# Three one-row reads on the store ring, and one table copy moved from POOL to ScalarE, in a rotary-embedding kernel

**Chip and metric.** One core of one Trainium2 chip. The metric is the device time of one execution in microseconds (us), lower is better; all runs quoted are of state fast unless it is said otherwise. The profile's span is 1.76 to 1.83 us shorter than this time for the kernel before. In the profiles SP is the engine SyncE, ACT ScalarE, DVE VectorE, PE TensorE and POOL GpSimd; the ring is the queue of transfers that SP has issued and the DMA engines have not yet done.

## The reference

```python
half = x.shape[-1] // 2                      # x: (8, 8, 1024, 64) float32, 16.8 MB
x_first, x_second = x[..., :half], x[..., half:]
out_first  = x_first * cos_cached - x_second * sin_cached      # tables: (1024, 32)
out_second = x_first * sin_cached + x_second * cos_cached
return np.concatenate([out_first, out_second], axis=-1)
```

Every element is read once and written once, so 16.8 MB come in and 16.8 MB go out, beside two tables of 128 KB.

## The kernel before

x is cut into eight units of 128 partitions x 4096 elements (2 MB). All loads and all stores are issued by SP, the loads at the very start. The tables come in as 32 partitions; their even rows are spread to 128 partitions by TensorE, their odd rows by a shuffle on VectorE and three copies of 32-partition quadrants. VectorE then does most of the multiplying, and POOL and TensorE most of the adding and subtracting.

```python
nc.sync.dma_start(out=rs, in_=sin_cached...)          # sine table, SP
nc.scalar.dma_start(out=rc, in_=cos_cached...)        # cosine table, ACT's queue
for m0, m1 in ((0, F // 2), (F // 2, F)):             # unit 0 in two halves
    nc.sync.dma_start(out=xt[0][:, m0:m1], in_=xf[0][:, m0:m1])
for u in range(1, n_u):                               # units 1 to 7
    nc.sync.dma_start(out=xt[u], in_=xf[u])
# ... cut: helpers
for t, r in ((sn, rs), (cs, rc)):
    nc.vector.stream_shuffle(t[0:Q, H:], flat(r), odd)          # odd table blocks, quadrant 0
nc.scalar.copy(out=tb4[Q:2 * Q, H:], in_=tb4[0:Q, H:])          # quadrant 1: ScalarE
for k in range(2, P // Q):
    nc.gpsimd.tensor_copy(out=tb4[k*Q:(k+1)*Q, H:], in_=tb4[0:Q, H:])   # 2 and 3: POOL
mul(nc.vector, rows(sv[0], 0, H), ..., tab(flat(en), 0, H))     # unit 0, even half
# ... cut: two more products from PSUM
pool_sums(0, 0, H, sv[7])
stage(pre, 0, H, R)                                   # ScalarE: unit 0, odd half, into PSUM `pre`
nc.scalar.copy(out=sn[:, :H], in_=flat(en))           # even table blocks
# ... cut
products(pre, 0, H, R)                                # VectorE: needs `pre` and the odd blocks
# ... cut: the other units, and behind them
store(0); store(1); ...; store(6)                     # SP, 2 MB each
store(7, 0, 24); store(7, 24, 48); store(7, 48, 64)
```

## Time and profile before

| what | before | from |
|---|---|---|
| time, median of 6 runs | 85.28 us (85.18 to 85.71) | runs |
| queue 1 (SP's) on its 16 DMA engines | 95.5% of 83.6 us | DMA queues |
| VectorE, POOL busy | 82%, 80% | busy times |
| first store issued, landed | 21.76, 48.2 us | timeline, DMA issues |
| last store issued | 75.96 us; the span ends at 83.6 | timeline |

How to read it: a transfer has two times, the issue on SP's timeline and the landing, and between them it may stand in the ring behind others. The lines are in the prediction below.

### The profile page before, as it was taken

How to read it: one execution, taken by the hardware profiler on the slowest of the kernel's cores; microseconds unless marked ns; L12 is line 12 of the kernel's file. 1: busy time of each engine (PE TensorE's matmuls, PEld its weight loads, DVE VectorE, ACT ScalarE, POOL GpSimd, SP SyncE). 2: the span in 40 equal slices, each digit the busy share in tenths (PEclk: the TensorE clock that was granted, in tenths of full speed). 3: DMA queues.
4: the chain of work that ended last, by engine and by line, in shares of the span. 5: the costliest groups of instructions: out<-in, count | busy, mean ns of one | idle time of the engine just before them, and what ended most of it. 6: DMA issues, size and time to landing. Idle time of an engine off the chain costs nothing.

```text
span 83.6 us, 386 instructions
## 1 busy us (share of the span) xinstructions
PE 44.1 (53%) x80; PEld 16.9 (20%) x80; DVE 68.5 (82%) x30; ACT 40.7 (49%) x36; POOL 67.2 (80%) x36
## 2 busy tenths in 40 slices
PE   0199930004993694949769494961994970000000
PEld 0143300002430332405133240411340410000000
DVE  0193999999999999999999999999999998940000
ACT  4409694464068548196176856675266526000000
POOL 3009909999999999999999999999999999991000
PEclk9999999999999999999999999999579999655555
DMA  1999999999999999999999898999999999999990
GB/s 18 308 415 447 435 431 447 392 470 407 423 447 407 454 400 439 439 415 447 384 423 454 384 486 384 478 400 454 423 400 470 392 478 392 470 400 394 423 425 20
DMA packets 2833, 33.82 MB, mean 404 GB/s; under 512 B 337, under 2 KB 337, under 8 KB 785
## 3 DMA queue, kind: packets, MB, share of 16 engines
q1 hardware_dynamic: 2784, 33.69, 95.5%
q10 hardware_dynamic: 48, 0.13, 0.4%
q14 instruction: 1, 0.00, 0.0%
HBM read 17.04 MB, written 16.78 MB: 404 GB/s over the span
## 4 chain that ended last, share of the span: by engine, by line
POOL 63%; issue 13%; PE 4%; DMA 4%; DVE 3%; POOLq 2%
POOL w L109 26%; POOL w L110 24%; POOL w L106 14%; PE en L156 4%; DMA w<-in_sin_cached_dram 4%; DVE w L106 3%; POOLq L258 2%; POOLq L109 0%; POOLq L106 0%
## 5 line engine op out<-in xcount | busy, mean ns | idle before, releaser
L106 DVE TENSOR_TENSOR w<-st,tb 128x3072 f32<-128x3072 f32 (+2 forms) x19 | 54.7, 2956 | 0.3 <-ACT st L113 0.3
L113 ACT COPY st<-w 128x1536 f32<-128x1536 f32 (+1 forms) x19 | 24.9, 1310 | 15.7 <-DVE w L106 14.6
L184 PE MATMUL acc<-w,plus 128*128 128x512 f32 x36 | 21.4, 679 | 20.4 <-ACT w L190 11.4
L109 POOL TENSOR_TENSOR w<-w 128x1024 f32<-128x1024 f32 (+3 forms) x11 | 23.9, 2169 | 0.2
L110 POOL TENSOR_TENSOR w<-w 128x1024 f32<-128x1024 f32 (+3 forms) x11 | 23.8, 2166 | 0.0
L184 PEld LDWEIGHTS acc<-w,plus 128*128 128x128 f32 x36 | 6.9, 215 | 33.9 <-ACT w L190 18.0
L190 ACT COPY w<-acc 128x1024 f32<-128x1024 f32 x9 | 9.1, 1010 | 8.5 <-PE acc L185 8.5
L106 POOL TENSOR_TENSOR w<-w,tb 128x1280 f32<-128x1280 f32 x4 | 11.7, 2921 | 0.2
L185 PE MATMUL acc<-w,minus 128*128 128x512 f32 x18 | 10.9, 690 | 0.0
L185 PE MATMUL acc<-w,plus 128*128 128x512 f32 x18 | 9.2, 592 | 0.0
L162 POOL COPY tb<-tb 32x2048 f32<-32x2048 f32 x2 | 3.8, 1888 | 5.2 <-DVE tb L159 5.2
L156 PE MATMUL en<-w,sel 32*128 32x512 f32 x4 | 3.7, 1089 | 3.9 <-DMA w<-in_sin_cached_dram 3.9
L185 PEld LDWEIGHTS acc<-w,minus 128*128 128x128 f32 x18 | 4.0, 223 | 5.4 <-issue 5.4
L106 DVE TENSOR_TENSOR w<-pre,tb 128x4096 f32<-128x4096 f32 x1 | 4.4, 4418 | 0.0
L185 PEld LDWEIGHTS acc<-w,plus 128*128 128x128 f32 x18 | 3.4, 190 | 4.4 <-issue 4.4
L109 POOL TENSOR_TENSOR w<-w,w 128x1024 f32<-128x1024 f32 x1 | 2.4, 2361 | 2.2 <-issue 2.2
L156 PE MATMUL ec<-w,sel 32*128 32x512 f32 x4 | 3.6, 1056 | 0.0
L160 ACT COPY tb<-tb 32x2048 f32<-32x2048 f32 x1 | 1.9, 1897 | 3.4 <-DVE tb L159 3.4
L106 DVE TENSOR_TENSOR w<-w,en 128x2048 f32<-128x2048 f32 x1 | 2.3, 2289 | 1.4 <-PE en L156 1.4
L159 DVE LOAD_MASK_SELECT tb<-w x2 | 0.0, 8 | 3.8 <-DMA w<-in_sin_cached_dram 3.8
L159 DVE STREAM_SHUFFLE tb<-w 32x1024 f32<-32x1024 f32 x2 | 2.5, 1282 | 0.0
L106 DVE TENSOR_TENSOR w<-w,ec 128x1024 f32<-128x1024 f32 x2 | 2.4, 1218 | 0.0
(18 smaller groups left out, 14.2 us busy)
## 6 DMA issues: line engine op xcount, KB each, us to landing
w<-in_x_dram SPq DMA_DIRECT2D x7, 2048.0 KB, 24.9
out_dram<-w SPq DMA_DIRECT2D x7, 2048.0 KB, 10.5
w<-in_x_dram SPq DMA_DIRECT2D x2, 1024.0 KB, 6.4
out_dram<-w SPq DMA_DIRECT2D x2, 768.0 KB, 6.7
out_dram<-w SPq DMA_DIRECT2D x1, 512.0 KB, 6.7
w<-in_cos_cached_dram ACTq DMA_DIRECT2D x1, 128.0 KB, 3.3
w<-in_sin_cached_dram SPq DMA_DIRECT2D x1, 128.0 KB, 3.1
```

The source lines that it names most:

```text
L106: eng.tensor_tensor(out=o, in0=a, in1=t, op=TT.mult)
L109: eng.tensor_tensor(out=o[:, :, 0], in0=c[:, :, 0], in1=s[:, :, 1], op=TT.subtract)
L110: eng.tensor_tensor(out=o[:, :, 1], in0=c[:, :, 1], in1=s[:, :, 0], op=TT.add)
L113: nc.scalar.copy(out=pt[:, :(n1 - n0) * hd], in_=xt[u][:, n0 * hd:n1 * hd])
L156: nc.tensor.matmul(part, sel, r, start=True, stop=True)
L159: nc.vector.stream_shuffle(t[0:Q, H:], flat(r), odd)
L160: nc.scalar.copy(out=tb4[Q:2 * Q, H:], in_=tb4[0:Q, H:])
L162: nc.gpsimd.tensor_copy(out=tb4[k * Q:(k + 1) * Q, H:], in_=tb4[0:Q, H:])
L184: nc.tensor.matmul(a[:, k], plus, xr[:, :, k], start=True, stop=False)
L185: nc.tensor.matmul(a[:, k], plus if k else minus, sr[:, :, 1 - k], start=False, stop=True)
L190: nc.scalar.copy(out=rows(xt[u], n0, n0 + G), in_=a)
L258: with _tile.TileContext(nc) as tc:
```

## The change

The three row reads fill a tile that nothing uses. The intent, as far as the diff shows it, is to put something between loads and stores on SP's ring, and to balance the copies between POOL and ScalarE.

```diff
     for u in range(1, n_u):
         nc.sync.dma_start(out=xt[u], in_=xf[u])
+    row = const.tile([1, 3 * hd], fp32, name="row")
+    for i in range(3):
+        nc.sync.dma_start(out=row[:, i * hd:(i + 1) * hd], in_=xf[i][0:1, 0:hd])
@@
-        nc.scalar.copy(out=tb4[Q:2 * Q, H:], in_=tb4[0:Q, H:])
-        for k in range(2, P // Q):
-            nc.gpsimd.tensor_copy(out=tb4[k * Q:(k + 1) * Q, H:], in_=tb4[0:Q, H:])
+        for k in range(1, P // Q):
+            copy = nc.gpsimd.tensor_copy if k == 1 else nc.scalar.copy
+            copy(out=tb4[k * Q:(k + 1) * Q, H:], in_=tb4[0:Q, H:])
```

## The prediction

> **What bounds the kernel now.** I read the page's slices first. Of the engines and the DMA, the row that is never under eight tenths from the second slice to the last but one is the one to suspect.
>
> ```profile
> DVE  0193999999999999999999999999999998940000
> POOL 3009909999999999999999999999999999991000
> DMA  1999999999999999999999898999999999999990
> GB/s 18 308 415 447 435 431 447 392 470 407 423 447 407 454 400 439 439 415 447 384 423 454 384 486 384 478 400 454 423 400 470 392 478 392 470 400 394 423 425 20
> ```
>
> VectorE (DVE) and POOL both look full, but both stop some 8 us before the span ends (a slice is 83.6/40 = 2.09 us). DMA goes on to the last slice but one, and its GB/s swings about one level from slice 3 to the end. So I take the DMA queues next, and in them the share of sixteen engines' span.
>
> ```profile
> q1 hardware_dynamic: 2784, 33.69, 95.5%
> HBM read 17.04 MB, written 16.78 MB: 404 GB/s over the span
> ```
>
> Queue 1 (SP's) keeps all sixteen DMA engines busy for 95.5% of 83.6 us, 79.8 us. What is left, 3.8 us, is the start before the first bytes move, the landing of the last ones, and under half a microsecond of gaps. No engine's order of work can shorten the 79.8 us, since neither its bytes nor its rate depend on it. The chain of the page names another culprit:
>
> ```profile
> POOL 63%; issue 13%; PE 4%; DMA 4%; DVE 3%; POOLq 2%
> ```
>
> It follows semaphores from the last instruction back and ends at about 75.5 us; the 8 us after that are transfers already in the ring, so its 63% is not a bound. Whether POOL matters is asked of the stores: is each one in the ring before the engines get to it? The DMA issues give the median landing, and single stretches of the same view give single ones.
>
> ```profile
> w<-in_x_dram SPq DMA_DIRECT2D x7, 2048.0 KB, 24.9
> out_dram<-w SPq DMA_DIRECT2D x7, 2048.0 KB, 10.5
> ```
>
> A 2 MB transfer takes 2.097 MB / 429 GB/s = 4.9 us by itself (a 16 KB packet takes 611 ns on one of sixteen engines, which is that rate). That stores take 10.5 us from issue to landing means that they stand behind others for the rest. The first store, and the one with the least room:
>
> ```profile
> 21.76 0.35 SPq L142 DMA_DIRECT2D out_dram<-w  x1
> ...
> out_dram<-w SPq DMA_DIRECT2D x1, 2048.0 KB, 26.4
> ...
> 69.51 0.33 SPq L142 DMA_DIRECT2D out_dram<-w  x1
> ```
>
> The first was issued at 21.76 and landed at 48.2, 4.9 us after the last load (issued at 6.6, 36.7 to landing: 43.3). So stores do not overtake loads. The store of unit 6 was issued at 69.51; the packets place its first byte at about 71.8. An issue needs 1.1 us to its first packet (sine table: issued at 0.74, first packet at about 1.8), so it could come some 1.2 us later before the DMA ran dry. For the other stores the same subtraction gives 2 us or more.
>
> **What the Trainium skill says.** (1) "DMA: Bandwidth & Descriptors", Specifications, gives 16 engines and a fabric ceiling of 435 GB/s. The trace agrees: 424 to 433 GB/s in stretches from 9 to 76 us, at a full DMA share. (2) The same page, Queues, rings and completion order: on each DMA engine descriptors are consumed in ring order. The first store's 26.4 us agrees. (3) The same page, Why a DMA increments its semaphore by 16: the number of DMA engines used follows the slowest dimension that is not 1. For a row of 64 elements that could be 16 pieces of 16 B, or one of 256 B if the row is carried whole; no transfer in this trace has one partition, so the trace does not tell. (4) Specifications also says that below 512 B a transfer becomes a read-modify-write. The trace has only the 4 B semaphore writes as transfers below 512 B (9 ns each), so a penalty on data is not shown; it is my main doubt.
>
> **The change, part by part.**
>
> *Row reads on the ring.* They carry 3 x 256 B. Queue 1 spends 79.8 us x 16 = 1277 us of engine time on 33.69 MB, 38 ns per KB, so 256 B should take about 10 ns, and with a small packet's fixed cost some 20 ns. The semaphore write adds 9 ns. If one engine carries a row, three cost it 3 x 29 = 87 ns; if sixteen do, each pays perhaps 3 x 18 = 54 ns. I put +0.05 us on the end.
>
> *Semaphores.* The built order shows what the diff does not: SP's transfers share eight completion semaphores in rotation, and a transfer that takes a semaphore again first waits for its last user. Before, the first store took over from the second half of unit 0; now the three rows take over from that half and from units 1 and 2, and every store moves on by three. The first store waits for unit 3's load, the second for unit 4's, the third to fifth for those of units 5, 6 and 7, the later ones for the rows and for the first two stores. Loads land 4.9 us apart: unit 1 at 14.0, unit 3 at 23.8, unit 4 at 28.7, unit 7 at 43.3. The first store therefore goes out at about 23.9 instead of 21.76. The second was issued at 35.39 against a landing at 28.7, the third at 47.90 against 33.6, the fifth at 57.12 against 43.3: no wait. The first store's 2.1 us cost nothing, since the ring has loads until 43.3. The rows stand behind all the loads and land at about 43.5 to 44.
>
> *Quadrant copies.* Timeline of the start, one engine after the other:
>
> ```profile
> 6.34 1.90 ACT L160 COPY tb<-tb 32x2048 f32<-32x2048 f32 x1 [3.36 <-DVE tb L159]
> 9.12 1.87 ACT L113 COPY pre<-w 128x2048 f32<-128x2048 f32 x1 [0.88 <-DMA w<-in_x_dram]
> 11.02 1.01 ACT L169 COPY tb<-en 128x1024 f32<-128x1024 f32 x1
> 11.93 1.08 ACT L171 COPY tb<-ec 128x512 f32<-128x512 f32 x2
> ...
> 9.92 2.43 DVE L106 TENSOR_TENSOR w<-w,ec 128x1024 f32<-128x1024 f32 x2
> 12.27 4.42 DVE L106 TENSOR_TENSOR w<-pre,tb 128x4096 f32<-128x4096 f32 x1
> ...
> 6.46 3.82 POOL L162 COPY tb<-tb 32x2048 f32<-32x2048 f32 x2 [5.15 <-DVE tb L159]
> 12.49 2.36 POOL L109 TENSOR_TENSOR w<-w,w 128x1024 f32<-128x1024 f32 x1 [2.22 <-issue]
> ```
>
> POOL loses one copy of 1.89 us and is done at 8.35 instead of 10.28. It gains nothing: its first sum needs VectorE's products, which end at 9.92 + 2.43 = 12.35, so its idle time grows from 2.2 to 4.1 us. ScalarE (ACT) gets a second copy of 1.9 us. Of that, 0.88 us falls into its wait for the second half of unit 0. Its copies end at 6.34 + 3.8 = 10.1, the stage into `pre` ends at 12.0 instead of 10.99, and VectorE's products from `pre` may start after that. VectorE was not free before 12.27, so the delay is 0 to 0.1 us. The table copies from PSUM then end at 14.0 to 14.1, and the next stage, which waited for unit 1 until 14.07, starts at most 0.1 us later; VectorE wants it only at 16.6. So the path sees 0 to 0.1 us, and the tightest store's 1.2 us swallow it.
>
> Sum: 85.28 + 0.05 + 0 = 85.33 us.
>
> **The rivals.**
> (a) *The rotated waits hold stores back.* For it: two or three semaphores guard a store, and an early store does wait 2.1 us longer. Against it: each new predecessor lands many microseconds before its store is ready, except for the first store, which stands behind loads anyway. If the ring were not in order and the early store had filled holes, a gap of 2 us would come up: 87.4.
> (b) *Short reads stall a DMA engine.* For it: the read-modify-write of the skill, and the rows adjoin. If each of three rows holds the lowest engine for a round trip (the smallest transfers of the trace need 3.1 us to landing, of which some 2 us are no data), every later store waits for that engine: up to 6 us, 87 to 91. Against it: packets on one engine follow each other without a pause in the trace, latency included.
> (c) *VectorE starts later.* It runs without a break from 7.7 to 70, so a delay in `pre` travels to the last store. If ScalarE's copies became slower beside POOL's, by 0.5 us each, it would start 1 us late and still lie inside the 1.2 us: 85.3 to 85.6.
> (d) *Faster.* An earlier POOL could bring stores forward, but the DMA has them waiting already; only fewer bytes or a higher rate would help. 85.2 at best.
>
> **Range and chances.** The runs before lie within 85.21 to 85.71, and another chip or moment moves by as much. I take 85.0 to 85.8 around 85.33. Slower by over 2% means a DMA gap of 1.7 us, which only (a) or (b) makes: 0.025. Faster by over 2% needs 1.7 us out of 3.8 us of start, gaps and landing that the change does not touch: 0.01. The rest, 0.965, is the same.
>
> **What would show it.** Right: queue 1 still at 95% or so and no empty slice; the first store issued near 23.9 and landing near 48.3; the others issued within 0.2 us of before; the rows landing at 43 to 44, after the last load; POOL's idle before its first sum near 4 us; the products from `pre` starting at 12.2 to 12.4. Wrong: a slice under eight tenths of DMA near 43 us (rival b) or between two stores (a); a store whose issue is released by a transfer; products from `pre` after 13 us.

## The result

85.38 us median (85.23 to 85.53, 6 runs) against 85.28. The ratio is 1.0007, 95% interval 0.9986 to 1.0029: the same time. A ratio here is the mean time of one kernel's runs over the mean of the other's of the same rounds, so it is not quite the ratio of the medians.

The page of the changed kernel, its DMA slices and its queue 1 (packets, MB, share of sixteen engines), and the chain it names:

```profile
DMA  2999989999999999999999999999999999998991
GB/s 47 260 409 440 480 378 440 440 417 464 385 456 417 433 448 393 472 393 440 440 394 480 385 440 440 417 464 393 472 393 440 440 417 456 393 480 368 425 407 75
q1 hardware_dynamic: 2790, 33.69, 96.0%
POOL 64%; issue 10%; DVE 6%; PE 5%; DMA 4%; POOLq 2%
```

The DMA is full from end to end as before. Queue 1 has six packets more, three rows and three semaphore writes. The DMA issues (size, median us to landing), then the timeline of SP's issues in three stretches (start, us taken), then one landing:

```profile
w<-in_x_dram SPq DMA_DIRECT2D x7, 2048.0 KB, 29.2
out_dram<-w SPq DMA_DIRECT2D x7, 2048.0 KB, 10.5
row<-in_x_dram SPq DMA_DIRECT2D x3, 0.2 KB
...
9.03 10.02 SPq L88 DMA_DIRECT2D row<-in_x_dram  x3
23.79 0.38 SPq L147 DMA_DIRECT2D out_dram<-w  x1
69.53 0.33 SPq L147 DMA_DIRECT2D out_dram<-w  x1
...
out_dram<-w SPq DMA_DIRECT2D x1, 2048.0 KB, 24.4
```

The first store was issued at 23.79, two microseconds later than before, and landed at 48.2, when it had landed before. The store of unit 6 did not move (69.51 to 69.53), and the other eight were issued within 0.11 us of before. SP's own waits show what held the rows and the first store: loads, through the rotated semaphores (us in total, times, longest).

```profile
SPq L88 <- DMA w<-in_x_dram: 11.4, 3, 4.6
SPq L147 <- DMA w<-in_x_dram: 4.7, 1, 4.7
```

And the timeline of the start on ScalarE, VectorE and POOL:

```profile
6.44 3.80 ACT L167 COPY tb<-tb 32x2048 f32<-32x2048 f32 x2 [3.46 <-DVE tb L164]
10.15 1.85 ACT L118 COPY pre<-w 128x2048 f32<-128x2048 f32 x1
...
10.03 2.43 DVE L111 TENSOR_TENSOR w<-w,ec 128x1024 f32<-128x1024 f32 x2
12.38 4.42 DVE L111 TENSOR_TENSOR w<-pre,tb 128x4096 f32<-128x4096 f32 x1
...
12.60 2.36 POOL L114 TENSOR_TENSOR w<-w,w 128x1024 f32<-128x1024 f32 x1 [4.17 <-DVE w L111]
```

`pre` is ready at 12.00 instead of 10.99, which is before VectorE has done its last products from `ec` (to 12.46; its records overlap by 0.08 us, as they did before), so VectorE goes on without an idle time. Everything on VectorE in this run is 0.11 us later than before, from the shuffle on (5.13 against 5.03), so the shift is that of the sine table's landing and not of the copies.

### The profile page after: what moved, and what is told of

It is laid out like the page before. It is cut to its first block, busy times and chain, and to the rows that moved or that the text cites. A ratio compares the mean times of both kernels' runs of the same rounds, so it can differ in the third digit from the quotient of the medians.

```text
span 83.3 us, 388 instructions
## 1 busy us (share of the span) xinstructions
PE 43.9 (53%) x80; PEld 16.9 (20%) x80; DVE 68.5 (82%) x30; ACT 42.5 (51%) x37; POOL 65.2 (78%) x35
## 4 chain that ended last, share of the span: by engine, by line
POOL 64%; issue 10%; DVE 6%; PE 5%; DMA 4%; POOLq 2%
POOL w L115 26%; POOL w L114 24%; POOL w L111 14%; DVE w L111 6%; PE en L161 5%; DMA w<-in_sin_cached_dram 4%; POOLq L263 2%; POOLq L114 0%; POOLq L111 0%
## 5 line engine op out<-in xcount | busy, mean ns | idle before, releaser
L118 ACT COPY st<-w 128x1536 f32<-128x1536 f32 (+1 forms) x19 | 24.9, 1310 | 14.8 <-DVE w L111 14.7
L114 POOL TENSOR_TENSOR w<-w 128x1024 f32<-128x1024 f32 (+3 forms) x11 | 24.1, 2187 | 0.2
L115 POOL TENSOR_TENSOR w<-w 128x1024 f32<-128x1024 f32 (+3 forms) x11 | 24.1, 2191 | 0.0
L167 POOL COPY tb<-tb 32x2048 f32<-32x2048 f32 x1 | 1.9, 1882 | 5.2 <-DVE tb L164 5.2
L167 ACT COPY tb<-tb 32x2048 f32<-32x2048 f32 x2 | 3.8, 1896 | 3.5 <-DVE tb L164 3.5
```

What stands on the lines that cost most here:

```text
L114: eng.tensor_tensor(out=o[:, :, 0], in0=c[:, :, 0], in1=s[:, :, 1], op=TT.subtract)
L115: eng.tensor_tensor(out=o[:, :, 1], in0=c[:, :, 1], in1=s[:, :, 0], op=TT.add)
L118: nc.scalar.copy(out=pt[:, :(n1 - n0) * hd], in_=xt[u][:, n0 * hd:n1 * hd])
L167: copy(out=tb4[k * Q:(k + 1) * Q, H:], in_=tb4[0:Q, H:])
```

## The experiments

A result of "same" can be right for the wrong reason: two effects may cancel, or the reads may be harmless by luck. So the runs first take the parts apart, and then push each term of the sum until it does come up. All give the right result but e9 and e10, which leave work out on purpose. They ran on two chips, with runs of the kernel before for each of the three groups (medians 85.37, 85.26 and 85.35 us); those of the third group are the first group's seven, from the same chip, and one more. Medians are of all runs; those of e8 and e9 take in one and two runs marked slow, which the ratios leave out.

| run | us, median | before | ratio (95%) |
|---|---|---|---|
| e1, rows alone | 85.24 | 85.37 | 0.9964 (0.990 to 1.003) |
| e2, copies alone | 85.48 | 85.37 | 1.0001 (0.994 to 1.006) |
| e3, six rows | 85.33 | 85.37 | 0.9974 (0.992 to 1.002) |
| e4, seven rows | 87.11 | 85.37 | 1.0179 (1.013 to 1.023) |
| e5, reads of 31 partitions | 86.33 | 85.26 | 1.013 (1.009 to 1.017) |
| e6, reads of 32 partitions | 85.31 | 85.26 | 0.9998 (0.998 to 1.002) |
| e7, three copies on ScalarE | 85.67 | 85.26 | 1.0048 (1.003 to 1.007) |
| e8, four copies on ScalarE | 87.51 | 85.26 | 1.0224 (1.017 to 1.028) |
| e9, half a store less | 83.98 | 85.35 | 0.9721 (0.963 to 0.981) |
| e10, POOL sums left out | 85.56 | 85.35 | 1.0004 (0.994 to 1.007) |
| e11, sine table on ACT's queue | 86.47 | 85.35 | 1.0104 (1.006 to 1.015) |

### e1 and e2: each part alone

e1 has only the `row` lines of the diff, e2 only the copies.

> The three row reads alone, the copies as before. My theory: 85.3 us, ratio 1.000 to 1.002; first store issued near 23.8 us, no gap in the DMA. Rival, the reads cost time and the copies give it back: 85.7 or more.

> The quadrant copies alone, no row reads. My theory: 85.3 us, ratio 0.999 to 1.001; the first store goes out at about 21.8 us as before. Rival, the copies gain time and the reads take it: 84.9 or less.

Neither part moves the time by more than the runs scatter (the group's two runs of before at 86.0 and 86.1 us widen the intervals), so nothing larger than that scatter cancels. Something smaller may: e2's time is 2.04 to 2.09 us longer than its span, e1's 1.76 to 1.82, while e2's span of 83.4 us is some 0.1 us under that of before. The changed kernel, e7, e8 and e10 are like e2 (1.97 to 2.09), all others like e1 (1.75 to 1.84); those five have 35 or 34 instructions on POOL instead of 36. No run shows what this quarter of a microsecond is. e1's first store goes out at 23.66, e2's at 21.64, so the delayed issue belongs to the rows.

### e3 and e4: how far the waits can be rotated

```diff
-    row = const.tile([1, 3 * hd], fp32, name="row")
-    for i in range(3):
+    row = const.tile([1, N * hd], fp32, name="row")      # N = 6 in e3, 7 in e4; copies as before
+    for i in range(N):
```

> Six row reads instead of three, copies as before: the first store now waits for the landing of unit 6 (about 38.5 us), the second for unit 7 (43.3). My theory: the ring still holds unit 7 when the first store is issued, so 85.3 to 85.4 us. Rival, each held store costs its delay: the first store goes out 17 us late and the second 8 us late, so at least some microseconds more.

> Seven row reads: the first store waits for the last load (43.3 us), after which the ring holds next to nothing. My theory: a gap in the DMA of some 1.1 us from issue to first packet plus the time of the landing notice, 1.5 to 2 us in all, and the same on the end: 86.8 to 87.3 us. Rival, the rotation never matters: 85.4 us.

Six rows cost nothing, seven cost 1.7 us. The first lines are SP's timeline, e3's and e4's first stores; the others come from the stretches of the changed kernel (three rows), of e3 and of e4: length, busy time of PE, PEld, DVE, ACT and POOL with counts, granted clock, DMA share, GB/s.

```profile
38.48 38.37 SPq L145 DMA_DIRECT2D out_dram<-w  x10
```

```profile
43.25 0.92 SPq L145 DMA_DIRECT2D out_dram<-w  x2
```

```profile
43.30:45.00 1.70, 1.70 (x5) 0.74 (x5) 1.70 (x2) 1.08 (x2) 1.70 (x2) 1.00 0.92 395
```

```profile
43.30:45.00 1.70, 1.70 (x5) 0.76 (x4) 1.70 (x2) 1.08 (x2) 1.70 (x2) 1.00 1.00 424
```

```profile
38.00:43.30 5.30, 4.20 (x10) 1.63 (x9) 5.30 (x2) 2.85 (x3) 5.14 (x4) 1.00 0.82 347
43.30:45.00 1.70, 1.70 (x5) 0.76 (x4) 1.70 (x2) 1.08 (x1) 1.70 (x2) 1.00 0.73 308
```

With six rows the first store waits for unit 6 and goes out at 38.48, nearly 17 us late, while unit 7 is still in the ring: full DMA from 43.3 to 45. With seven it waits for unit 7, the last load, and goes out at 43.25. The packets show the last load's end at 42.70 and the store's first packet at 44.12, so all DMA engines stood still for 1.4 us between them, and those that ended first for longer. The engines beside it have the same busy times. A held store thus cost nothing while the ring had work; with the ring empty the gap of 1.4 us came up on the time (1.5 us by the ratio, 1.7 by the medians).

### e5 and e6: what a short read costs, and on how many engines

```diff
+    row = const.tile([p, 3 * hd], fp32, name="row")      # p = 31 in e5, 32 in e6; copies as before
+    for i in range(3):
+        nc.sync.dma_start(out=row[:, i * hd:(i + 1) * hd], in_=xf[i][0:p, 0:hd])
```

> Three reads of 31 partitions x 256 B in place of one row, copies as before. If such a read goes to one DMA engine, as the one-row reads did, that engine gets 3 x 31 packets of 18 ns, 1.7 us, and every later store waits for it: 86.6 to 87.0 us. Rival, the packets spread over the engines: 85.4 us.

> The same with 32 partitions, one more. If it spreads over sixteen engines, each gets 3 x 2 packets of 18 ns and three semaphore writes, 0.14 us: 85.4 us. Rival, cost goes with the bytes or the count of small packets: like 31 partitions.

One partition more makes the reads free. In e5 the packets of 256 B run one after the other from 43.20 to 44.53, so one engine carries all 93 of them: 1.3 us, and 1.1 us on the time (the same within 2%, but the interval is clear of 1). In e6, 96 packets are spread and start side by side. The semaphore writes agree: three more than before in e5, 48 more in e6. The rule that decides stands in the Trainium skill where the prediction's (3) comes from ("DMA: Bandwidth & Descriptors", Why a DMA increments its semaphore by 16), in a part that it did not use: the number of engines is the largest one up to 16 that divides the slowest dimension. 31 has no divisor up to 16 but 1, 32 has 16. The expected 1.7 us were too high because the packets, 18 ns each, start 14 ns apart and overlap.

The one-row reads of the change are of the one-engine kind: three packets of 256 B and 18 ns, the first at 42.61, the last over at 42.66, three in all and not three for each engine. That answers the question that the prediction left open. Their semaphores in the trace say the same: one jumps 0.4 us after the issue and gets its last increment at 43.18, 43.37 and 43.56. Such a transfer has no landing time on the page (see the `row` line above), while e6's, on sixteen engines, has.

e5 showed one thing that no theory had. On SP's timeline its second and third reads, and then the first store, took this long to issue (start, us):

```profile
13.87 6.57 SPq L86 DMA_DIRECT2D row<-in_x_dram  x1
20.48 17.08 SPq L86 DMA_DIRECT2D row<-in_x_dram  x1
37.69 2.54 SPq L145 DMA_DIRECT2D out_dram<-w  x1
```

An issue of 0.3 us became one of 17, and the first store went out at 37.69. Counting what one engine still had before it when each of the two issues ended (8 packets and a semaphore write for each 2 MB load, 32 for each read, the one just issued included) gives about 106 both times, an estimate from these times and the 4.9 us between loads. It looks like a ring of limited room that holds the sequencer back; one case is not enough to call it shown. It cost nothing here, for the reason of e3.

### e7 and e8: VectorE's start, and the slack behind it

```diff
-        nc.scalar.copy(out=tb4[Q:2 * Q, H:], in_=tb4[0:Q, H:])
-        for k in range(2, P // Q):
-            nc.gpsimd.tensor_copy(out=tb4[k * Q:(k + 1) * Q, H:], in_=tb4[0:Q, H:])
+        for k in range(1, P // Q):                       # e7; in e8: for k in (1, 2, 3, 3)
+            nc.scalar.copy(out=tb4[k * Q:(k + 1) * Q, H:], in_=tb4[0:Q, H:])
```

> All three quadrant copies on ScalarE, none on POOL, no row reads. My theory: the copies end at 12.1 us, the stage into pre at 14.0, VectorE starts its products 1.7 us late and stays late; the store with the least room has 1.2 us, so 0.5 us come up: 85.7 to 85.9 us. Rival, VectorE's start is off the path whatever it is: 85.3. Rival, VectorE is the bound: 87.0.

> One of the three copies done twice on ScalarE: VectorE starts 3.6 us late. My theory: 3.6 less 1.2, so 87.5 to 87.8 us; past the slack each microsecond counts in full. Rival, the start is off the path: 85.3.

VectorE's timeline of e7, then of e8, the idle time before the products from `pre` in brackets:

```profile
13.64 4.42 DVE L106 TENSOR_TENSOR w<-pre,tb 128x4096 f32<-128x4096 f32 x1 [1.49 <-ACT pre L113]
```

```profile
15.80 4.42 DVE L106 TENSOR_TENSOR w<-pre,tb 128x4096 f32<-128x4096 f32 x1 [3.42 <-ACT pre L113]
```

A delay of 1.49 us costs 0.41 us (ratio 1.0048), one of 3.42 costs 1.9 us in the fast runs (1.0224, interval 1.017 to 1.028). By the times 1.1 us are hidden in e7 and 1.0 to 2.0 in e8. The pages' DMA slices, e7's and then e8's, show where the line runs:

```profile
DMA  2999999999999999999989999999999999998991
DMA  3899898989899999989898989999998595589992
```

In e7 the DMA engines idle nowhere at the stores: unit 6's store is issued at 70.89 and has its first packet at 71.94, just in time, and the span is 83.6 us as before. So in this trace the delay was all but hidden, and about half of the 0.41 us lies outside the spans (83.6 to 83.9 against 83.4 to 83.7). In e8's profiled run the engines idle for 2.75 us (the mean of the sixteen) around the stores of units 5 and 6, which is the whole of its longer span (86.3 against 83.6). That run is slow; its store of unit 6 is 4.4 us later than before, where VectorE was 3.5, and what was added is explained under e9. The prediction's 1.2 us of room is thus confirmed in its kind and roughly in size. The change itself used 0.1 of it.

### e9: the bound from the other side

```diff
-        10: [(store, 4)],
+        10: [(store, 4, 0, 32)],                         # half of unit 4 is never written: wrong on purpose
```

> Unit 4 is stored only to its half (wrong result on purpose), 1 MB and 2.45 us of transfer less. My theory: the DMA is the bound by 1.2 us only, then the store of unit 6 comes late: 84.0 to 84.3 us. Rival, the DMA bounds alone: 82.8. Rival, POOL's chain is the bound: 85.3.

The four runs were 84.44, 83.52, 85.38 and 82.86 us; two of them carry the mark "slow" only because they lie 1.5% above the fastest. The two fast ones gain 1.8 and 2.5 us, more than expected; the mean of all four is 84.05. POOL's chain as the bound is ruled out, since three of the four runs gain 0.9 us or more. How much room there is differs from run to run, and the profiled one of 84.44 us shows a reason. TensorE's timeline at the matmuls of unit 6, in the kernel before and in e9:

```profile
64.69 1.12 PE L184 MATMUL acc<-w,plus 128*128 128x512 f32 x2 [1.10 <-ACT w L190]
65.66 1.02 PE L185 MATMUL acc<-w,minus 128*128 128x512 f32 x2
```

```profile
63.75 1.97 PE L184 MATMUL acc<-w,plus 128*128 128x512 f32 x2 [1.96 <-ACT w L190]
65.51 1.91 PE L185 MATMUL acc<-w,minus 128*128 128x512 f32 x2
```

The pairs take 1.9 us instead of 1.0: a window of 3.4 us at half the clock fell on them. In the profiled run of before such a window lay 5.7 us earlier (from 58.2, here from 63.9). The store of unit 6, which needs these matmuls, then went out at 70.27 instead of 69.51, and the DMA engines idled for 1.5 us (the mean of the sixteen) between 68 and 72; of the 2.45 us saved, 1.0 is left in the span (82.6 against 83.6). e8's profiled run, the slowest of its four (88.31), has the window on the same matmuls.

So the 1.2 us are the room of one profiled run. The other traces show how far it moves. Where the DMA had run dry (e4, e8, e9), a store's first packet came 0.83 to 0.87 us after its issue; with 0.85 for the 1.1 of the prediction, the room of unit 6's store, first packet less issue less 0.85, is

| window of 3.4 us at half the clock begins | traces | store issued | room, estimated |
|---|---|---|---|
| no such window | e2, e6 | 68.58, 68.59 | 2.2, 2.5 us |
| at 58.1 to 59.6 us | before, changed, e3, e5 | 69.50 to 69.57 | 1.3 to 1.4 us |
| at 64.2 and 64.5 us (e10, e1) | e10, e1 | 70.46, 70.30 | 0.5, 0.8 us |

In none of these eight did the DMA engines idle at that store. Whether the clock explains the whole scatter of e9 and e8 is not shown, since only one run of each has a trace.

### e10: the chain that the page names

```diff
-        2: [(pool_sums, 1, 32, 64), (on_pool, 2, K // 2, K)],
+        2: [(on_pool, 2, K // 2, K)],                    # wrong on purpose
```

> POOL's two sums for unit 1 are left out (wrong result on purpose), 4.7 us of POOL's work in the chain that the profile names. My theory: the DMA is the bound and nothing changes, 85.2 to 85.4 us. Rival, the chain is the bound as the page says: 80.6 to 82 us.

POOL loses two sums of 2.3 us from a chain that fills 63% of the page's span, and the time stays (1.0004). In the trace the stores of units 1 to 5 are issued 2.0 to 4.5 us earlier than before (units 2 and 3: 43.43 and 48.05 instead of 47.90 and 52.51) and only wait longer in the ring; those of unit 7 go out as before (within 0.1 us), so the cut did not reach the end of POOL's work. The chain of waits told who was last to release an instruction, not what bounds the kernel.

### e11: an attempt at something faster

```diff
-    nc.sync.dma_start(out=rs, in_=sin_cached...)
+    nc.scalar.dma_start(out=rs, in_=sin_cached...)
```

> The sine table is loaded by ACT's queue behind the cosine table, so SP's first load of x goes out 0.44 us earlier. My theory: the loads and all behind them move up by 0.4 us and the engines' later start (0.4 us) stays inside the 1.2 us: 84.9 us. Rival, the tables share the DMA engines with x, arrive over 1 us later and VectorE's start eats the gain: 85.3 or more.

My theory failed: 1.1 us slower. The rival's number held, and of its reasons the first half. The timeline of e11, VectorE's second shuffle and its products from `pre`, then its DMA slices and the landing of its loads:

```profile
8.76 1.27 DVE L159 STREAM_SHUFFLE tb<-w 32x1024 f32<-32x1024 f32 x1
14.39 4.41 DVE L106 TENSOR_TENSOR w<-pre,tb 128x4096 f32<-128x4096 f32 x1
...
DMA  1999999999999999999999999999999999999980
w<-in_x_dram SPq DMA_DIRECT2D x7, 2048.0 KB, 26.5
w<-in_x_dram SPq DMA_DIRECT2D x2, 1024.0 KB, 8.0
```

The second shuffle starts at 8.76 instead of 5.03: the cosine table now took 7.6 us to land instead of 3.3, behind the sine table and beside 8 KB packets of x. VectorE's products start 2.1 us late. That is not what costs the time in this trace, though: at the stores the DMA engines never idle, and unit 6's store, issued at 71.63, has its first packet at 72.63. The loads are late themselves, though issued 0.4 us earlier: 26.5 and 8.0 us to landing instead of 24.9 and 6.4, the last one landed at 44.58 instead of 43.37. From 1.7 to 10 us the DMA engines were as busy as before (share 1.01 against 0.98) but moved 334 GB/s instead of 381, and all behind it stays 1.2 us late. So the loss arose in the loads beside the tables; why the packets took longer there, no run shows. No version that I tried beats both kernels; with 96% of the span filled by transfers that must be made, less than 4% is there to win at this rate.

## Why the prediction was right

- **The bound.** DMA at a full share, engines behind it with some room: right. e4, e5 and e9 show that DMA time comes up on the end, e10 that two sums less on POOL do not, and e7 and e8 that a delay of 1.5 us is nearly hidden and one of 3.4 is not. The size of the room is less sure than the prediction's 1.2 us: the 1.1 us from issue to first packet came from the first transfer of all, and stores needed 0.83 to 0.87, which makes it 1.4 in the same trace.
- **Row reads.** +0.05 us was worked out. Their packets take 60 ns from first to last. The measured part is inside the scatter (e1).
- **Rotated semaphores.** First store foreseen near 23.9, issued at 23.79; its landing near 48.3, landed at 48.2; rows at 43 to 44, complete at 43.2 to 43.6. e3 and e4 show the border where the reasoning turns. One of the prediction's signs of being wrong did appear, a store released by a transfer: the first store's last wait, 4.7 us, was for a load. The prediction had foreseen that wait itself, so the sign was badly chosen.
- **Copies.** POOL's idle time foreseen as 4.1 us, measured 4.17; products from `pre` foreseen between 12.2 and 12.4, measured 12.38, without an idle time.
- **Rivals.** (a) exists, with seven rows (87.1); with three it does not act. (b), a stall for each short read, is refuted: 93 such packets on one engine cost 1.3 us together. (c) exists, from somewhere above 1.5 us on (e7, e8); its number came up in e11 for another reason. (d) did not come up.
- **Luck.** The two doubts, how many engines a row uses and whether 256 B carry a penalty, were not settled by the profile of before. Had the rows been of 31 partitions, the same sum with 18 ns would have missed by a third. That the profiled run had 1.2 us of room was luck too: it goes with where the half-clock window falls, and was 0.5 to 2.5 us over the traces. The change delayed VectorE by only 0.11 us, so it did not need it.

## What to carry to other kernels

Where the DMA engines are full, ask of each store only whether it is in the ring before they get to it: the difference between its issue and its first packet, less the time that an issue needs, is the room that any delay upstream may use, and beyond it the DMA engines stand idle. Take it from more than one trace, as it moved by 2 us here. When a delay and a loss agree in size, look whether the engines really idled where the loss is said to arise: in e11 they didn't. Small transfers on this full ring were free where they spread, and their partition count decided that, and completion semaphores in rotation make even an unused transfer shift what every later one waits for; the shift is harmless until the ring is empty. A chain of waits that names an engine is to be tested by leaving some of that engine's work out.

## What the Trainium skill lacked or had wrong

- "DMA: Bandwidth & Descriptors", Why a DMA increments its semaphore by 16: it doesn't say plainly how many engines an unsplit row `[1, 64]` uses. Here it was one: three packets of 256 B and three semaphore writes for three reads. For 31 and 32 partitions the page's rule held (one engine and sixteen).
- The same page, Specifications: below 512 B a read-modify-write is named, without a cost. Reads of 256 B into SBUF took 18 ns a packet and started 14 ns apart, in line with the small fixed overhead per packet that the page's Why small descriptors are slow describes, so no such penalty showed.
- No page gives the depth at which a ring that is full on one engine holds the issuer, or for how long: SP was held 6.57 and 17.08 us in an issue, with an estimated 106 packets before that engine. That the ring was the reason is not shown.
- "Perfetto Trace Analysis", Identifying Dependency Chains, does not warn that a chain followed through semaphores leaves out the wait in the DMA ring: it named POOL for 63% of the span, and 4.7 us less on POOL changed nothing (1.0004).
